# A two-layer streaming encoder in float32: output products of the feed-forward groups issued later, and silu of the gate in one ScalarE instruction

## The chip, the cores and the metric

The kernel runs on one core of one Trainium2 chip. A core has five engines, each with its own queue of instructions that it works through in order: TensorE (PE in the profile; its weight loads are PEld), VectorE (DVE), ScalarE (ACT), GpSimd (POOL) and SyncE (SP), which here only issues DMA transfers. The engines wait for each other by semaphores. The metric is the device time of one execution in microseconds (us), lower is better. The runs of one kernel here lie within 1.1% of each other.

## The reference

All products are in float32 with an accuracy that one pass of the fast format of TensorE does not give, so the kernel makes three products of high and low parts for each. What is computed, for two layers, with x of 512 tokens by 1024:

```
for i in range(DEPTH):                       # 2
    xn = rmsnorm(x, norm1_g[i])
    proj = xn @ w_in[i]                      # 1024 x 6144
    u_pool, q, k, v, g_a, g_b = split(proj)
    o = diff_attention(rotary(rmsnorm(q)), rotary(rmsnorm(k)), v, lam)   # chunk-causal, 4 heads of 2 parts
    attn_out = rmsnorm(o, subln_g[i]) * (1 - lam_init)
    pool_out = pool_mixer(u_pool, pool_w[i], pool_scale[i])              # windowed means, 4 groups
    merged = sigmoid(g_a) * pool_out + sigmoid(g_b) * attn_out
    x = x + merged @ w_out[i]                # 1024 x 1024
    hn = rmsnorm(x, norm2_g[i])
    gate, up = split(hn @ w_ffn_in[i])       # 1024 x 5632
    x = x + (silu(gate) * up) @ w_ffn_out[i] # 2816 x 1024
```

The parts that the change touches are the last three lines, the product with `w_out` ahead of them, and the first lines of the second layer.

## The kernel before

**High and low parts.** Each float32 operand is split into a high part in the fast format and the rest (`split`: ScalarE casts `whi`, VectorE subtracts to `wlo`). A product is three matmuls, high by high, high by low and low by high (`three`, `product`, `in_turn`; L280 to L282 and L299 to L301), each 128 by 128 by 512. Weights come in pieces of 512 KB (`raw`, 7 buffers), and their parts lie in 6 buffers each. With `by_dma`, `parts` makes the low part without VectorE: ScalarE writes minus the high part (L235), and a GpSimd DMA adds the weights to it (L236).

**The residual** `res` lies transposed, 8 rows of tiles by 512 tokens. `add_out` (L685) adds a finished product in PSUM to it.

**Feed-forward.** The 2816 hidden columns are 22 blocks of 128. The last two make the odd group (`odd_group`); the other 20 make five groups of four (`GROUPS`). A group computes its gate and up products by a scheme of seven products instead of eight (`PRODUCTS`, in the order 1, 5, 6, 2, 7, 4, 3), in which sums and differences of weights are made on VectorE (L860 for product 5, L866 and L867 for 6, L880 for 3). Products 1 and 2 add up in the banks named `sc`, 5 and 3 in `tr`, 6 and 7 in `mm`; 4 is in `sc` again. Each product is 24 matmuls.

**Hidden activations.** After products 2, 7, 4 and 3 `Hidden.put` makes h = silu(gate) * up for two tiles of 128 tokens: ScalarE takes tanh of half the normalised gate (`th`, L782), VectorE forms (th + 1) * gate (L783) and multiplies by up and by the factor of the tokens (`h`, L784). Since tokens stand on partitions there and the next product needs hidden columns on partitions, `turned` transposes: VectorE turns blocks of 32 (L314), one DMA writes them to HBM (`away`, L315), four DMAs read them back in place (`near`, L317). `back` splits `near` into `fh` (ScalarE) and `fl` (VectorE). It is emitted by `later`, after a delay in columns of matmuls (`HIDDEN_AWAY`), or at the latest when `need` asks for it. The delays and the order of the code set the order of each queue; the framework's scheduler may move an instruction up where its operands are free.

**Output units.** An output unit is a quarter of the product of a group's hidden activations with `w_ffn_out` (`pair_units`), or a half of the odd group's (`odd_units`): 24 matmuls as well, in two halves whose banks are `oy` and `mm` in turn. Units of a group are issued between the products of the next one, behind products 6, 2, 7 and 4 (`FILLED`); in the last group only two are, and the other two and the last group's four follow at the end. `weight_plan` lists the pieces of weights in the same order, since SyncE loads them in that order.

**Around it.** `last_out` ends the product with `w_out` in four steps, each followed by `Sets.put`, which prepares the input of the feed-forward (`xg`, `xh`, `xl`, and squares `sq`). In the second layer the first attention block needs the root mean square of each token, `token_stats`: VectorE adds the squares, eight tiny matmuls with ones sum them over partitions (L412), and a few small operations follow. It stands behind the first of four products with the weights of q and k.

Of the kernel before, what the change touches and what calls it, by code (L numbers as in the profile page):

```python
# [13 lines left out]
AF = mybir.ActivationFunctionType  # L14
ALU = mybir.AluOpType
# [7 lines left out]
NT = S // P  # L23
# [18 lines left out]
LOADS = {1: ((0, 0),), 5: ((1, 0), (1, 4)), 2: ((0, 4),), 4: ((1, 4),)}  # L42
FILLED = (6, 2, 7, 4)
ODD = 20
# [8 lines left out]
QK_AWAY, SCORE_AWAY, PROB_AWAY, AV_AWAY, MERGE_AWAY = 28000, 26000, 32000, 18000, 24000  # L53
HIDDEN_AWAY = 22000


def weight_plan():
# [22 lines left out]
    for layer in range(L):  # L80
# [24 lines left out]
        for g, f0 in enumerate(GROUPS):  # L105
            for n in PRODUCTS:
                for q in LOADS.get(n, ()):
                    for h in range(2):
                        quarter(f0, *q, h)
                if n in FILLED:  # L110
                    at = FILLED.index(n)
                    if not g:
                        if at < 2:
                            block("w_ffn_out", layer, span((512 * at, 512)), ODD, ODD + 2)
                    elif g < len(GROUPS) - 1 or at < 2:
                        out(GROUPS[g - 1], (at,))
        out(GROUPS[-2], (2, 3))
        out(GROUPS[-1], range(4))
# [4 lines left out]
def trunk_kernel(  # L123
# [278 lines left out]

    def token_stats(full):

# [4 lines left out]
        squares[0] = None  # L409
        ss = mm_ps()[:, :NT]  # L410
        for t in range(NT):
# [60 lines left out]
    for layer in range(L):  # L472
# [14 lines left out]
        def attention(j, before, then):  # L487
# [88 lines left out]
            if not at_start:  # L576
                w = wblock(KD)
            for t in range(NT):
                if at_start:
                    acc = first_acc[t]  # L580
                    first_products(t, steps[2] + steps[3])
                    if not t:
                        token_stats(True)
                else:
                    acc = mm_ps()
                    product(acc, list(zip(x_tok(t), w)))
                    if layer and not t and j == ORDER[0]:
                        token_stats(True)
                qn = sb.tile([P, 4, QK], F32, name="qn", tag="qn", bufs=3)
                ss = small("ss4", 4)  # L590
                for h in range(4):
                    nc.scalar.activation(qn[:, h, :], acc[:, h * QK:(h + 1) * QK], AF.Square, accum_out=ss[:, h:h + 1])
                r = rsqrt_mean(ss, QK, 4, (QK ** -0.5, 1.0), [stats[0][:, i, t:t + 1] for i in (3, 4)])
                for h in range(4):
                    g = qkg[layer][:, h // 2 * QK:(h // 2 + 1) * QK]
                    nc.vector.scalar_tensor_tensor(
                        qn[:, h, :], acc[:, h * QK:(h + 1) * QK], r[:, h:h + 1], g, op0=ALU.mult, op1=ALU.mult)
                rotate(qn, t)
                if not at_start:
                    qn = turned(qn.rearrange("p h c -> p (h c)"), 4, "qn", 3)  # L600
                later(17400 + 5700 * t if at_start else QK_AWAY, lambda t=t, qn=qn: turn(t, qn))
                if not t and then is not None:
                    then()
# [149 lines left out]
        def last_out(x):  # L753
            for i in range(4):
                w = piece(4, True)
                for a in range(2):
                    acc = mm_ps()
                    in_turn(acc, [(cols(w, a)[2 * n + h], (ms[j][0][:, h, :], ms[j][1][:, h, :]))
                                  for n, j in enumerate(ORDER[2:]) for h in range(2)])
                    add_out(i + 4 * a, acc)  # L760
                x.put(i)
# [3 lines left out]
        class Hidden:  # L765
# [9 lines left out]
            def put(self, half, t, gate, up):  # L775

                if half not in self.h:
# [3 lines left out]
                th = sb.tile([P, VD], F32, name="th", tag="mt", bufs=3)  # L781
                nc.scalar.activation(th, gate, AF.Tanh, scale=stats[0][:, 2, n:n + 1])  # L782
                nc.vector.scalar_tensor_tensor(th, th, 1.0, gate, op0=ALU.add, op1=ALU.mult)  # L783
                nc.vector.scalar_tensor_tensor(  # L784
                    h[:, :, t, :], th.rearrange("p (i c) -> p i c", i=2), stats[0][:, 5, n:n + 1],
                    up.rearrange("p (i c) -> p i c", i=2), op0=ALU.mult, op1=ALU.mult)
                if t:
# [9 lines left out]
        def odd_group(x):  # L797
            to = Hidden(ODD, *HIDDEN_AT[ODD])
            w = [piece(2, True) for _ in range(4)]
            accs = [mm_ps(), mm_ps(), tr_ps(), tr_ps()]  # L800
# [40 lines left out]
        def group(g, x):  # L841
# [8 lines left out]
            def prepare(n):  # L850
# [4 lines left out]
                elif n == 5:  # L855
                    raws[21], raws[1] = got
                    sets[5] = []
                    for h in range(2):
                        s1, r21 = raws[1][h][0], raws[21][h][0]
                        nc.vector.tensor_add(s1, r21, s1)  # L860
                        sets[5].append(parts(s1))
# [30 lines left out]
            for n in PRODUCTS:  # L892
# [36 lines left out]
                elif n == 3:  # L929
                    multiply(3, c, False)  # L930
                    for t in range(2):
                        nc.vector.tensor_add(x2[t], c[t], x2[t])
                        to[0].put(1, t, x2[t][:, :VD], x2[t][:, VD:])
                if n in FILLED:
                    at = FILLED.index(n)
                    if not g:
                        if at < 2:
                            odd_units(at)
                    elif g < len(GROUPS) - 1 or at < 2:
                        pair_units(GROUPS[g - 1], at)  # L940

# [31 lines left out]
        for g in range(len(GROUPS)):  # L973
            group(g, sets_of_x)
        for i in (2, 3):
            pair_units(GROUPS[-2], i)
# [59 lines left out]
```

## Time and profile before

| | us |
|---|---|
| median of 3 runs | 1509.73 (1505.37 to 1521.37) |
| the profiled execution | 1509.37 |
| its span, first to last instruction | 1507.6 |
| ScalarE busy / VectorE busy | 700.9 / 1059.6 |
| mean clock granted to TensorE | 0.967 of full speed |

The profiled execution is one run taken by the hardware profiler. A row of a group of instructions gives the line of the code, the engine, the operation with what it writes and reads, how often it ran, and its mean time. A row of a wait gives who waited for whom, the total, how often, and the longest. A row of the timeline gives start, duration and, in brackets, the engine's idle time just before and what ended it. Busy time of TensorE is modelled from the starts of pipelined matmuls; a matmul of 512 columns shows as 0.39 us but the next one starts 0.23 us later.

### The profile page before, as it was taken

The page shows a single profiled execution, that of the slowest core. Times are in us where ns is not written, and L with a number is a line of the kernel's source. Part 1 is how long each engine was busy: PE and PEld are TensorE (multiplying, and loading weights), DVE is VectorE, ACT ScalarE, POOL GpSimd, SP SyncE. Part 2 cuts the span into 40 slices and gives each one's busy share as a digit, 9 for nine tenths or more (in the row PEclk, how much of TensorE's full clock was granted, in tenths as well). Part 3 has the DMA queues.
Part 4 walks back from the last instruction along what each step waited for, and adds up shares of the span by engine and source line. Part 5 has one row for each costly group of instructions (what it writes and reads, how often), then busy time and mean ns, then how long its engine had stood idle before and what let it go on. Part 6 is the DMA issues. An engine that isn't in the chain of part 4 may idle for free.

```text
span 1507.6 us, 18715 instructions
## 1 busy us (share of the span) xinstructions
PE 1414.3 (94%) x6242; PEld 1156.8 (77%) x6242; DVE 1059.6 (70%) x2055; ACT 700.9 (46%) x1310; POOL 129.0 (9%) x151
## 2 busy tenths in 40 slices
PE   9999999997888989898899999999998989898898
PEld 7888888886776867677678888888876767686686
DVE  7778687856756767575667797878576667585763
ACT  6453353455534444454344443535574443553540
POOL 1001000010100000000011101000110000000000
PEclk9999999998989999999999999999999999999999
DMA  8344444465666675757525454445566666757652
GB/s 291 100 141 138 145 138 131 146 155 139 150 171 194 171 205 149 218 158 211 160 65 159 121 178 159 126 133 158 147 154 167 175 187 169 216 149 222 159 162 84
DMA packets 145392, 241.30 MB, mean 160 GB/s; under 512 B 41360, under 2 KB 88976, under 8 KB 145296
## 3 DMA queue, kind: packets, MB, share of 16 engines
q1 hardware_dynamic: 133056, 198.14, 41.1%
q0 software_dynamic: 10944, 39.85, 14.4%
q10 hardware_dynamic: 1296, 2.12, 0.5%
q8 instruction: 49, 0.80, 0.2%
q14 instruction: 47, 0.39, 0.1%
HBM read 210.82 MB, written 29.23 MB: 159 GB/s over the span
## 4 chain that ended last, share of the span: by engine, by line
PE 64%; DMA 15%; DVE 11%; ACT 4%; issue 3%; SPq 2%; POOL 0%; ACTq 0%; DVEq 0%; POOLq 0%
PE mm L299 12%; PE mm L300 12%; PE mm L301 12%; DMA near<-away 8%; DMA away<-near 5%; DMA raw<-in_wts 3%; PE mm L280 3%; PE mm L281 3%; PE mm L282 3%; DVE wlo L211 2%; PE oy L280 2%; PE oy L281 2%; SPq L317 2%; PE oy L282 2%; PE sc L280 2%
## 5 line engine op out<-in xcount | busy, mean ns | idle before, releaser
L210 ACT CAST whi<-raw 128x1024 fp32r<-128x1024 f32 (+1 forms) x229 | 238.1, 1046 | 219.8 <-PE mm L281 87.5
L211 DVE TENSOR_TENSOR wlo<-raw,whi 128x1024 fp32r<-128x1024 f32 (+1 forms) x229 | 275.5, 1210 | 39.0 <-ACT whi L210 38.3
L299 PE MATMUL mm<-whi,xh 128*128 128x512 f32 x480 | 189.9, 396 | 0.0
L301 PE MATMUL mm<-whi,xl 128*128 128x512 f32 x480 | 188.2, 392 | 0.0
L300 PE MATMUL mm<-wlo,xh 128*128 128x512 f32 x480 | 188.1, 392 | 0.0
L280 PE MATMUL oy<-fh,whi 128*128 128x512 f32 (+1 forms) x180 | 80.2, 446 | 65.6 <-ACT fh L210 62.9
L236 POOL DMA_DIRECT2D wlo<-in_wts x76 | 66.6, 876 | 676.8 <-ACT wlo L235 631.4
L301 PEld LDWEIGHTS mm<-whi,xl 128*128 128x128 f32 x480 | 90.7, 189 | 19.4
L300 PEld LDWEIGHTS mm<-wlo,xh 128*128 128x128 f32 x480 | 90.9, 189 | 17.6
L299 PEld LDWEIGHTS mm<-whi,xh 128*128 128x128 f32 x480 | 90.9, 189 | 17.6
L685 DVE TENSOR_TENSOR res<-mm,res 128x512 f32<-128x512 f32 x96 | 65.0, 681 | 53.2 <-PE mm L282 49.0
L333 POOL TENSOR_TENSOR r<-r,mhalf 128x4 f32<-128x4 f32 (+1 forms) x64 | 58.0, 906 | 515.6 <-DVE r L332 442.6
L300 PE MATMUL mm<-xl,whi 128*128 128x512 f32 x256 | 99.8, 390 | 0.0
L299 PE MATMUL mm<-xh,whi 128*128 128x512 f32 x256 | 99.8, 390 | 0.0
L301 PE MATMUL mm<-xh,wlo 128*128 128x512 f32 x256 | 99.6, 389 | 0.0
L280 PEld LDWEIGHTS oy<-fh,whi 128*128 128x128 f32 x180 | 38.6, 215 | 79.4 <-ACT fh L210 68.0
L234 ACT CAST whi<-raw 128x1024 fp32r<-128x1024 f32 x76 | 79.3, 1043 | 37.5 <-PE mm L281 35.4
L280 PE MATMUL sc<-whi,xh 128*128 128x512 f32 x240 | 93.6, 390 | 0.0
L282 PE MATMUL sc<-whi,xl 128*128 128x512 f32 x240 | 93.4, 389 | 0.0
L281 PE MATMUL sc<-wlo,xh 128*128 128x512 f32 x240 | 93.4, 389 | 0.0
L235 ACT ACTIVATE wlo<-raw 128x1024 fp32r<-128x1024 f32 x76 | 80.4, 1057 | 25.1 <-PE sc L281 8.6
L281 PE MATMUL oy<-fl,whi 128*128 128x512 f32 (+1 forms) x180 | 79.4, 441 | 0.2 <-DVE fl L211 0.2
(241 smaller groups left out, 3188.9 us busy)
## 6 DMA issues: line engine op xcount, KB each, us to landing
raw<-in_wts SPq DMA_DIRECT2D x264, 512.0 KB, 4.5
wlo<-in_wts POOLq DMA_DIRECT2D x76, 512.0 KB, 8.1
away<-near SPq DMA_DIRECT2D x72, 256.0 KB, 2.2
near<-away SPq DMA_DIRECT2D x288, 64.0 KB, 2.7
away<-near SPq DMA_DIRECT2D x28, 128.0 KB, 1.7
near<-away SPq DMA_DIRECT2D x112, 32.0 KB, 2.4
res<-in_x_t SPq DMA_DIRECT2D x4, 512.0 KB, 7.0
pwr<-in_pool_w ACTq DMA_DIRECT2D x8, 256.0 KB, 2.7
```

The costliest lines, as they stand in the source:

```text
L210: ins = nc.scalar.copy(hi, src)
L211: nc.vector.tensor_sub(lo, src, hi.bitcast(F32))
L234: nc.scalar.copy(hi, raw)
L235: nc.scalar.activation(lo, raw, AF.Copy, scale=-1.0)
L236: nc.gpsimd.dma_start(lo.rearrange("p a b -> p (a b)"), wts[piece_no], accum_op=ALU.add)
L280: nc.tensor.matmul(acc, lhsT=ah, rhs=bh, start=start, stop=False, **check)
L281: nc.tensor.matmul(acc, lhsT=ah, rhs=bl, start=False, stop=False, **check)
L282: last = nc.tensor.matmul(acc, lhsT=al, rhs=bh, start=False, stop=stop, **check)
L299: nc.tensor.matmul(acc, lhsT=ah, rhs=bh, start=i == 0, stop=False)
L300: nc.tensor.matmul(acc, lhsT=ah, rhs=bl, start=False, stop=False)
L301: last = nc.tensor.matmul(acc, lhsT=al, rhs=bh, start=False, stop=i == n - 1)
L685: return nc.vector.tensor_add(res[d][:, cs], acc, res[d][:, cs])
```

## The change

Six things change.

- Output units are placed by a table, `UNITS`, from the place (group number, product) to the units issued behind it; source -1 is the odd group. Units of group g now begin behind product 4 of group g + 1, and the last two are issued behind products 1 and 5 of group g + 2. The odd group's are behind products 7 and 4 of the first group. At the end all four units of the last but one group and the four of the last stand in a row. `weight_plan` follows.
- `HIDDEN_AWAY` is 42000 columns, not 22000.
- `put` takes silu in one ScalarE instruction, and one VectorE operation multiplies by up and by the factor. ScalarE's table of functions is loaded where silu begins and where exp comes back.
- The pieces of `last_out`, and two of four of the odd group, are split by ScalarE and VectorE, without the GpSimd DMA.
- The first sums of weights in group 0 (L860) are ordered behind the last `add_out` of `last_out`.
- In layer 1 `token_stats` stands behind the second product, in a bank `sc`, and the first tile is evicted after it.

```diff
-FILLED = (6, 2, 7, 4)
+UNITS = {(0, 7): [(-1, 0)], (0, 4): [(-1, 1)], (1, 4): [(0, 0)], (1, 3): [(0, 1)],
+         (2, 1): [(0, 2)], (2, 5): [(0, 3)], (2, 4): [(1, 0)], (2, 3): [(1, 1)],
...
-HIDDEN_AWAY = 22000
+HIDDEN_AWAY = 42000
...
-        out(GROUPS[-2], (2, 3))
+        out(GROUPS[-2], range(4))
...
-    def token_stats(full):
+    def token_stats(full, bank=mm_ps):
...
-        ss = mm_ps()[:, :NT]
+        ss = bank()[:, :NT]
...
-                    if layer and not t and j == ORDER[0]:
-                        token_stats(True)
+                    if layer and j == ORDER[0] and t < 2:
+                        held.append((t, acc))
+                        if not t:
+                            continue
+                        token_stats(True, s_ps)
+                        evicted(*held.pop(0))
+                evicted(t, acc)
...
-                w = piece(4, True)
+                w = piece(4)
...
-                    add_out(i + 4 * a, acc)
+                    x.added = add_out(i + 4 * a, acc)
...
-                nc.scalar.activation(th, gate, AF.Tanh, scale=stats[0][:, 2, n:n + 1])
-                nc.vector.scalar_tensor_tensor(th, th, 1.0, gate, op0=ALU.add, op1=ALU.mult)
+                nc.scalar.activation(th, gate, AF.Silu, scale=stats[0][:, 1, n:n + 1])
                 nc.vector.scalar_tensor_tensor(
-                    h[:, :, t, :], th.rearrange("p (i c) -> p i c", i=2), stats[0][:, 5, n:n + 1],
-                    up.rearrange("p (i c) -> p i c", i=2), op0=ALU.mult, op1=ALU.mult)
+                    h[:, :, t, :], up.rearrange("p (i c) -> p i c", i=2), stats[0][:, 1, n:n + 1],
+                    th.rearrange("p (i c) -> p i c", i=2), op0=ALU.mult, op1=ALU.mult)
...
-            w = [piece(2, True) for _ in range(4)]
+            w = [piece(2, k % 2 > 0) for k in range(4)]
...
-                        nc.vector.tensor_add(s1, r21, s1)
+                        with ExitStack() if g else tc.issue_after(x.added.ins):
+                            nc.vector.tensor_add(s1, r21, s1)
...
-                if n in FILLED:
-                    at = FILLED.index(n)
-                    if not g:
-                        if at < 2:
-                            odd_units(at)
-                    elif g < len(GROUPS) - 1 or at < 2:
-                        pair_units(GROUPS[g - 1], at)
+                for source, i in UNITS.get((g, n), ()):
+                    if source < 0:
+                        odd_units(i)
+                    else:
+                        pair_units(GROUPS[source], i)
```

Where instructions stand in the built programs, at three places. The line numbers of the new kernel are up to ten higher.

TensorE's queue, a middle group of layer 0, around the first output unit on the hidden part that was finished last. Before, behind product 6 (`mm<-...xr`):

```order
L280 MATMUL mm<-whi,xrh 128x512
L281 MATMUL mm<-wlo,xrh 128x512
L282 MATMUL mm<-whi,xrl 128x512
L280 MATMUL oy<-fh,whi 128x512
L281 MATMUL oy<-fl,whi 128x512
L282 MATMUL oy<-fh,wlo 128x512
```

and now, behind product 4 (`sc<-...x`):

```order
L281 MATMUL sc<-whi,xh 128x512
L282 MATMUL sc<-wlo,xh 128x512
L283 MATMUL sc<-whi,xl 128x512
L281 MATMUL oy<-fh,whi 128x512
L282 MATMUL oy<-fl,whi 128x512
L283 MATMUL oy<-fh,wlo 128x512
```

The unit moved down by products 2, 7 and 4 and by two units of the group before.

VectorE's queue, a middle group of layer 0, from the work behind product 3 to the first evictions of units (`res<-oy`, `res<-mm`). Before:

```order
L211 TENSOR_TENSOR fl<-near,fh 128x512
L314 STREAM_TRANSPOSE near<-h 128x4x4x32
L211 TENSOR_TENSOR wlo<-raw,whi 128x1024 x2
L880 TENSOR_TENSOR raw<-raw 128x1024 x2
L211 TENSOR_TENSOR wlo<-raw,whi 128x1024 x2
L211 TENSOR_TENSOR fl<-near,fh 128x512
L906 TENSOR_TENSOR cqn<-mm,cta 128x512 x2
L211 TENSOR_TENSOR wlo<-raw,whi 128x1024
L685 TENSOR_TENSOR res_85<-oy,res_85 128x512
```

and now, from the unit behind product 3 to those behind products 1 and 5:

```order
L695 TENSOR_TENSOR res_86<-mm,res_86 128x512
L876 TENSOR_TENSOR raw<-raw 128x1024
L212 TENSOR_TENSOR wlo<-raw,whi 128x1024
L877 TENSOR_TENSOR raw<-raw 128x1024
L212 TENSOR_TENSOR wlo<-raw,whi 128x1024 x2
L212 TENSOR_TENSOR fl<-near,fh 128x512
L695 TENSOR_TENSOR res_87<-oy,res_87 128x512
L695 TENSOR_TENSOR res_87<-mm,res_87 128x512
L890 TENSOR_TENSOR raw<-raw 128x1024 x2
L212 TENSOR_TENSOR wlo<-raw,whi 128x1024
L695 TENSOR_TENSOR res_88<-oy,res_88 128x512
```

The `fl` of product 3's hidden part stood ahead of the first sums of product 6; now it stands ahead of the eviction of the unit behind product 1.

VectorE's queue in `last_out` of layer 0, from the first eviction on. Before:

```order
L685 TENSOR_TENSOR res_85<-mm,res_85 128x512
L860 TENSOR_TENSOR raw<-raw 128x1024
L211 TENSOR_TENSOR xl<-xg,xh 128x512
L685 TENSOR_TENSOR res_87<-mm,res_87 128x512
L717 TENSOR_TENSOR xg<-xg 128x256
```

and now:

```order
L695 TENSOR_TENSOR res_85<-mm,res_85 128x512
L212 TENSOR_TENSOR xl<-xg,xh 128x512
L695 TENSOR_TENSOR res_87<-mm,res_87 128x512
L212 TENSOR_TENSOR wlo<-raw,whi 128x1024
L727 TENSOR_TENSOR xg<-xg 128x256
```

L860 (now L870) left the place behind the first eviction; it follows the last one of `last_out`, and a split of a piece of the odd group's weights stands among the evictions.

More of the change, by code (lines that the diff above doesn't have):

```diff
@@ L109, in weight_plan @@
                         quarter(f0, *q, h)
-                if n in FILLED:
-                    at = FILLED.index(n)
-                    if not g:
-                        if at < 2:
-                            block("w_ffn_out", layer, span((512 * at, 512)), ODD, ODD + 2)
-                    elif g < len(GROUPS) - 1 or at < 2:
-                        out(GROUPS[g - 1], (at,))
-        out(GROUPS[-2], (2, 3))
+                for source, i in UNITS.get((g, n), ()):
+                    if source < 0:
+                        block("w_ffn_out", layer, span((512 * i, 512)), ODD, ODD + 2)
+                    else:
+                        out(GROUPS[source], (i,))
+        out(GROUPS[-2], range(4))
         out(GROUPS[-1], range(4))
@@ L577, in attention, with evicted @@
                 w = wblock(KD)
[L578 to L582, printed above, removed]
-                        token_stats(True)
-                else:
-                    acc = mm_ps()
-                    product(acc, list(zip(x_tok(t), w)))
-                    if layer and not t and j == ORDER[0]:
-                        token_stats(True)
+            held = []
+            def evicted(t, acc):
                 qn = sb.tile([P, 4, QK], F32, name="qn", tag="qn", bufs=3)
@@ L601, in attention @@
                 later(17400 + 5700 * t if at_start else QK_AWAY, lambda t=t, qn=qn: turn(t, qn))
+            for t in range(NT):
+                if at_start:
+                    acc = first_acc[t]
+                    first_products(t, steps[2] + steps[3])
+                    if not t:
+                        token_stats(True)
+                else:
+                    acc = mm_ps()
+                    product(acc, list(zip(x_tok(t), w)))
+                    if layer and j == ORDER[0] and t < 2:
+                        held.append((t, acc))
+                        if not t:
+                            continue
+                        token_stats(True, s_ps)
+                        evicted(*held.pop(0))
+                evicted(t, acc)
                 if not t and then is not None:
@@ L933, in group @@
                         to[0].put(1, t, x2[t][:, :VD], x2[t][:, VD:])
[L934 to L937, printed above, removed]
-                            odd_units(at)
-                    elif g < len(GROUPS) - 1 or at < 2:
-                        pair_units(GROUPS[g - 1], at)
+                for source, i in UNITS.get((g, n), ()):
+                    if source < 0:
+                        odd_units(i)
+                    else:
+                        pair_units(GROUPS[source], i)
         def next_x(i):
@@ L974, in trunk_kernel @@
             group(g, sets_of_x)
-        for i in (2, 3):
+        for i in range(4):
             pair_units(GROUPS[-2], i)
```

2 rows, old and new, of the table UNITS are left out of this document.

## The prediction

> **What bounds the kernel now.** I read the page first, then TensorE's own waits, then the clock just behind each of them, then the chain of waits at two places.
>
> ```profile
> span 1507.6 us, 18715 instructions
> ...
> PE 1414.3 (94%) x6242; PEld 1156.8 (77%) x6242; DVE 1059.6 (70%) x2055; ACT 700.9 (46%) x1310; POOL 129.0 (9%) x151
> ```
>
> TensorE is busy 94% of the span, so 1507.6 - 1414.3 = 93 us of idle time is one thing to win. The other hides inside "busy": after a wait the granted clock falls, and the matmuls behind it take longer. The waits of TensorE alone (total, how often, longest; the smaller ones left out add to 6.4 us):
>
> ```profile
> PE oy L280 <- ACT fh L210: 62.9, 12, 7.6
> PE mm L280 <- DVE res L685: 12.1, 4, 8.5
> PE mm L412 <- DVE sq L408: 2.9, 1, 2.9
> PE oy L280 <- DVE res L685: 2.7, 2, 1.7
> PE tr L280 <- DVE cqn L932: 2.5, 5, 0.8
> ```
>
> So one kind of wait, an output unit waiting for the hidden activations `fh`, makes two thirds of the idle time. What the clock adds I read from stretches of 7 us that start where TensorE resumes (columns: stretch, busy time and count by engine, then the granted clock, DMA share, GB/s):
>
> ```profile
> core 0: us, PE busy (x) PEld busy (x) DVE busy (x) ACT busy (x) POOL busy (x), PEclk, DMA share, GB/s
> 357.90:364.90 7.00, 7.00 (x23) 5.65 (x24) 6.97 (x12) 6.65 (x11) 0.53 (x1) 0.72 0.00 0
> 418.46:425.46 7.00, 7.00 (x20) 5.31 (x21) 2.27 (x4) 0.00 (x0) 0.00 (x0) 0.66 0.18 75
> ...
> 767.75:774.75 7.00, 7.00 (x21) 5.84 (x22) 3.12 (x15) 0.00 (x0) 2.05 (x2) 0.51 0.00 0
> 1109.67:1116.67 7.00, 7.00 (x25) 5.68 (x26) 6.97 (x12) 6.65 (x11) 0.55 (x1) 0.78 0.27 60
> ...
> 1431.99:1438.99 7.00, 7.00 (x20) 5.32 (x21) 3.70 (x5) 0.90 (x1) 0.00 (x0) 0.64 1.01 347
> 1481.60:1488.60 7.00, 6.78 (x28) 5.36 (x29) 2.05 (x3) 0.00 (x0) 0.00 (x0) 1.00 0.10 37
> ```
>
> TensorE is "busy" for all 7 us, yet at clock 0.64 it issues 20 matmuls. A stretch at clock c loses (1 - c) x 7 us. Eleven stretches follow long waits for `fh` (first 418.46, last 1431.99) and lose 25.8 us together, 2.35 each; the twelfth wait, 2.0 us before 1481.60, left the clock at 1.00. The two behind `res` (357.90, 1109.67) lose 3.5 us, the one behind `sq` (767.75) 3.4 us.
>
> **Why the units wait.** The pace: product 6 of a group has eight triples, from the first row here to one pitch behind the second, 5.44 us for 24 matmuls. An output unit has 24 as well.
>
> ```profile
> 405.27 0.39 PE L280 MATMUL mm<-whi,xrh 128*128 128x512 f32 x1
> ...
> 410.03 0.39 PE L280 MATMUL mm<-whi,xrh 128*128 128x512 f32 x1
> ```
>
> The chain of one group (rows of TensorE, SyncE and VectorE, and the chain of waits between them):
>
> ```profile
> 597.17 0.47 PE L280 MATMUL tr<-whi,xth 128*128 128x512 f32 x1 [0.66 <-DVE cqn L932]
> 601.99 0.70 DVE L314 STREAM_TRANSPOSE near<-h 128x512 f32<-128x512 f32 x1
> 602.72 0.34 SPq L315 DMA_DIRECT2D away<-near  x1
> 606.77 6.29 DMA near<-away
> 613.16 0.63 ACT fh L210
> 613.81 0.69 DVE L211 TENSOR_TENSOR fl<-near,fh 128x512 fp32r<-128x512 f32 x1 [1.50 <-ACT fh L210]
> 613.83 0.79 PE L280 MATMUL oy<-fh,whi 128*128 128x512 f32 x1 [4.87 <-ACT fh L210]
> ```
>
> Product 5 could start at 597.17 - 0.66 = 596.51, so product 1 began, and product 3 of the group before ended, at 591.07. Its hidden part is ready at 613.79, 22.7 us later: 11.6 us in VectorE's queue, 10.4 us in two DMA passes, the rest on ScalarE. Between product 3 and the unit lie products 1, 5 and 6, 16.3 us. Where product 5 does not wait (first row below) the same sum gives 16.3 + 5.2 = 21.5 us. The other two rows are waits at the end of layer 0 and of the kernel:
>
> ```profile
> 545.00 0.80 PE L280 MATMUL oy<-fh,whi 128*128 128x512 f32 x1 [5.22 <-ACT fh L210]
> 734.13 0.80 PE L280 MATMUL oy<-fh,whi 128*128 128x512 f32 x1 [4.00 <-ACT fh L210]
> 1481.60 0.50 PE L280 MATMUL oy<-fh,whi 128*128 128x512 f32 x1 [2.02 <-ACT fh L210]
> ```
>
> **The change, part by part.**
>
> Units later. In the groups with all four units the first unit on a group's hidden part moves from behind product 6 (16.3 us after product 3) to behind product 4; between lie units, too: 1, unit, 5, unit, 6, 2, 7, 4, so 8 x 5.44 = 43.5 us against a need of 21.5 to 22.7. The odd group's units move behind products 7 and 4: five products, 27.2 us; the longest wait, 7.6 us past 16.3, means a need of 23.9. At the end four units instead of two cover the last group: 21.8 us against 4.0 us beyond two units and a 1.7 us wait in layer 0, 16.6. All twelve waits go: -62.9, and with them -25.8 of clock. The waits for `cqn` (-2.5) and for `res` at the last units (-2.7) go as well: a unit now lies between product 3 and the next group's product 1, and between 1 and 5.
>
> What is late next: VectorE. Its order puts `fl` of product 3 ahead of the eviction of the unit behind product 1, whose bank `oy` the unit behind product 5 writes. That unit starts 21.8 us after product 3 (unit, 1, unit, 5); before it must lie `fl` 0.69 and the eviction, about 0.7, so `fh` must end by 20.4. It took 21.5 to 22.7: a wait of 1.1 to 2.3, if nothing of the chain gets shorter, in three groups of each layer. Ends: 0 (the loads by accumulation of product 2 are now issued behind `fh`, no longer beside its DMA) to 6.6 each, if `away` takes 5.1 more, as the slow one here against the median:
>
> ```profile
> 402.96 7.30 DMA away<-near
> ...
> away<-near SPq DMA_DIRECT2D x72, 256.0 KB, 2.2
> ```
>
> I take 1.5 x 6 = +9.0, nearest to the measured chain, with no clock price, since 2.0 us had none.
>
> Last output products before the feed-forward. The wait of 8.46 us is no shortage of weights:
>
> ```profile
> 339.28 16.02 DMA raw<-in_wts
> ...
> 355.42 1.23 DVE L860 TENSOR_TENSOR raw<-raw 128x1024 f32<-128x1024 f32 x1 [13.41 <-DMA raw<-in_wts]
> ...
> 357.90 0.79 PE L280 MATMUL mm<-mh,whi 128*128 128x512 f32 x1 [8.46 <-DVE res L685]
> ```
>
> VectorE stands at L860 for a load that landed at 355.3, with the evictions behind it; the new order puts L860 behind the last eviction. Gone: all four waits of this kind, -12.1, and -3.5 of clock. Twelve pieces of weights are split by VectorE, not by a second ScalarE pass and an accumulating DMA:
>
> ```profile
> L211 DVE TENSOR_TENSOR wlo<-raw,whi 128x1024 fp32r<-128x1024 f32 (+1 forms) x229 | 275.5, 1210 | 39.0 <-ACT whi L210 38.3
> L235 ACT ACTIVATE wlo<-raw 128x1024 fp32r<-128x1024 f32 x76 | 80.4, 1057 | 25.1 <-PE sc L281 8.6 <-ACT wlo L235 7.4 <-PE sc L282 2.0
> wlo<-in_wts POOLq DMA_DIRECT2D x76, 512.0 KB, 8.1
> ```
>
> VectorE +12 x 1.21 = 14.5 us, ScalarE -12.7, and 12 DMAs of 512 KB less. Six fall in each layer, 7.3 us, under the 13.4 us for which VectorE stood at L860 in layer 0; cost 0, at most 14.5 if that cover is gone.
>
> Silu. Each layer has 11 hidden pairs with four `put`s each, so 88 of L783 go; ScalarE's instruction keeps its form, and three table loads come (silu, exp, silu):
>
> ```profile
> L782 ACT ACTIVATE th<-cta,stats x20: 508/510/512, 452.5 to 1465.2; 128x256 f32<-128x256 f32 x20
> L783 DVE SCALAR_TENSOR_TENSOR th<-th,cta x20: 378/416/422, 454.0 to 1466.6; 128x256 f32<-128x256 f32 x20
> L375 ACT ACT_TABLE_LOAD  x1: 1283/1283/1283, 1.2 to 1.2; - x1
> 545.00:613.80 68.80, 62.95 (x264) 50.70 (x264) 45.70 (x62) 30.92 (x39) 5.20 (x6) 0.95 0.67 183
> ```
>
> 88 x 0.416 = 36.6 us off VectorE, which is busy 45.7 of 68.8 us in a group: off the path, gain 0, at best 0.8 us per chain (two in a row) where the chain still binds. The loads: 0 to 3 x 1.28 = 3.8; ScalarE is busy 30.9 of 68.8 us, so 0. The Trainium skill, page "ScalarE: Activation LUTs", section "What ACT_TABLE_LOAD costs", speaks against the change here: a switch of set costs the load and a drain, 2.66 us together; our row agrees on the 1283 ns of the load and shows no drain. By that page the three would be up to 8.0 us, and the sum 1411 instead of 1403.
>
> Start of layer 1. The sums of squares are ready 2.92 us after the first product; now a second product (5.44 us) runs first: -2.9 and -3.4 of clock. The price is bank pressure: the first product's bank must be free before the fourth starts, one product after the statistics. Its last reader ends at 773.5 in this row, 5.8 us after they started at 767.75; one product and the statistics themselves (1.5 us) take 6.9: cost 0, at most 2.
>
> ```profile
> 767.75 1.45 PE L412 MATMUL mm<-ones,sq 128*128 128x1 f32 x7 [2.92 <-DVE sq L408]
> 772.40 1.13 DVE L596 SCALAR_TENSOR_TENSOR qn<-mm,r,hg 128x128 f32<-128x128 f32 x4 [1.19 <-POOL r L333]
> ```
>
> The longer delay (42000 for 22000 columns, 18.6 for 9.7 us at 5.44 per 12288) sends the splits to ScalarE later, where it stood long for `near` already; nothing on TensorE asks for them sooner than above: 0.
>
> **The sum.** 62.9 + 25.8 + 2.5 + 2.7 + 12.1 + 3.5 + 2.9 + 3.4 = 115.8. Span 1507.6 - 115.8 + 9.0 = 1400.8; the profiled execution took 1509.37, 1.8 more than its span, so 1402.6, say 1403. The median of the three runs, 1509.73, is the same within 0.4.
>
> **Rivals.**
> - The wait moves to VectorE's queue in full: `fh` ends 5.1 us later than before, six waits of 6.6 with 2.35 of clock, 53.7 instead of 9.0: 1447. For it: a group at full pace takes 11 x 5.44 = 59.8 us for the DMA work of 68.8 (0.67 x 68.8 = 46.1, a share of 0.77). Against: part of that traffic now comes later.
> - The move does nothing for the units: each `fh` is emitted later and stands in ScalarE's queue until its new unit waits as long. Then only 12.1 + 3.5 + 2.9 + 3.4 = 21.9 goes: 1487. Against: 43.5 us of work for a chain of 22.7.
> - The other side, slower: DMA becomes the bound in the groups. Behind the waits the engines run at share 1.01 and 347 GB/s, so they can be filled. The ten groups would then last as long as their DMA work; since 21.9 us are won elsewhere, it decides at 68.8 + 2.2 = 71.0 us a group, 54% more than the 46.1 us of now. At 72 us the time is 1509 + 32 - 22 = 1519. No row here shows packets that much slower.
>
> **How the numbers follow.** Forecast (below 1420) 0.74, the VectorE rival (1420 to 1460) 0.17, units unmoved 0.04, DMA bound 0.02, several of these that cancel to within 1% 0.03. The range goes from 1389 (no residual wait, 1391.8 + 1.8, and most of the 6.4 us of small waits gone) to 1440, into the first rival. A measurement of this kernel tells some 1% from no change; faster by more 0.95, within 0.03, slower 0.02.
>
> **What would show it.** Right: no TensorE wait for `fh` above 2 us; mean clock above 0.985 for 0.967; the wait of `mm` for `res` gone; groups of about 60 us; no wait for `sq`. The residual shows as `oy` waiting for `res`, three times a layer. Wrong: waits for `fh` or `res` of over 4 us with clock 0.64 behind them, a DMA share near 1 through whole groups, or TensorE waiting for `wlo`, `th` or `h`.

## The result, and the profile after

| | before | after |
|---|---|---|
| median, us | 1512.1 (4 runs, 1505.4 to 1521.4) | 1404.1 (4 runs, 1400.3 to 1410.5) |
| profiled execution, us | 1509.4 | 1400.3 |
| its span, us | 1507.6 | 1398.5 |

The ratio is 0.929, with a 95% interval from 0.922 to 0.935: the changed kernel is faster by 108 us. Forecast were 1403 us for the profiled execution, 1389 to 1440. The profiled execution of the changed kernel is the fastest of its four.

The head of the page of the changed kernel (span, busy time of each engine, granted clock in 40 slices):

```profile
span 1398.5 us, 18612 instructions
...
PE 1375.9 (98%) x6242; PEld 1137.6 (81%) x6242; DVE 1045.0 (75%) x1979; ACT 693.4 (50%) x1301; POOL 117.7 (8%) x139
...
PEclk9999999999999999999999999999999999999999
```

Two sums explain the gain. TensorE's idle time fell from 93.3 to 1398.5 - 1375.9 = 22.6 us, 70.7 less. Its busy time, with the same 6242 matmuls, fell by 38.4 us: the matmuls that ran at a low clock behind the waits are at full clock now. The forecast had 74.1 less for the waits (83.1 less the 9.0 that it expected to remain) and 32.7 for the clock.

TensorE's two largest waits in the changed kernel (total us, how often, longest; no other kind adds up to more than 1.7 us):

```profile
PE oy L281 <- DVE res L695: 9.6, 6, 2.5
PE mm L300 <- DVE qn L589: 3.5, 2, 2.4
```

No wait for `fh` is left, none for `sq`, and none of `mm` for `res`. The two rows are what stands in their place. The columns of the next view are those of the prediction's stretches; it has one middle group of layer 0 and the same of layer 1:

```profile
547.03:606.87 59.84, 59.84 (x265) 49.57 (x264) 43.45 (x56) 31.39 (x38) 5.24 (x6) 1.00 0.78 215
...
1247.00:1307.00 60.00, 60.00 (x266) 49.70 (x265) 44.95 (x58) 31.75 (x40) 5.21 (x6) 1.00 0.78 215
```

A group lasts 59.84 us, which is eleven blocks of 24 matmuls at 5.44 us; TensorE is busy for all of it at full clock. The DMA share rose from 0.67 to 0.78, where the first rival had worked out 0.77, and the passes of the chain hardly felt it: the medians from issue to landing are 2.4 us for an `away` DMA (2.2 before) and 2.1 us for a `near` one (2.7 before).

```profile
away<-near SPq DMA_DIRECT2D x72, 256.0 KB, 2.4
near<-away SPq DMA_DIRECT2D x288, 64.0 KB, 2.1
```

The engines beside TensorE still wait for the hidden parts, only nobody waits for them: ScalarE stands 83.2 us for `near`, VectorE 46.9 us at `fl`.

```profile
ACT fh L211: 83.2, 25
DVE fl L212: 46.9, 20
```

### The profile page after: what moved, and what is told of

Its sections match the earlier page's. It is cut to its first block, busy times and chain, and to the rows that moved or that the text cites. A ratio compares the mean times of both kernels' runs of the same rounds, so it can differ in the third digit from the quotient of the medians.

```text
span 1398.5 us, 18612 instructions
## 1 busy us (share of the span) xinstructions
PE 1375.9 (98%) x6242; PEld 1137.6 (81%) x6242; DVE 1045.0 (75%) x1979; ACT 693.4 (50%) x1301; POOL 117.7 (8%) x139
## 4 chain that ended last, share of the span: by engine, by line
PE 81%; DMA 7%; DVE 6%; ACT 2%; issue 1%; SPq 1%; POOL 1%; ACTq 0%; DVEq 0%; POOLq 0%
PE mm L300 13%; PE mm L302 12%; PE mm L301 12%; PE mm L282 6%; PE mm L283 5%; PE mm L281 5%; DMA away<-near 4%; PE oy L281 2%; PE oy L282 2%; PE oy L283 2%; PE sc L281 2%; PE sc L282 2%; PE tr L282 2%; PE tr L283 2%; PE tr L281 2%; PE sc L283 2%
## 5 line engine op out<-in xcount | busy, mean ns | idle before, releaser
L211 ACT CAST whi<-raw 128x1024 fp32r<-128x1024 f32 (+1 forms) x241 | 250.9, 1048 | 197.9 <-PE mm L282 56.8
L212 DVE TENSOR_TENSOR wlo<-raw,whi 128x1024 fp32r<-128x1024 f32 (+1 forms) x241 | 291.3, 1212 | 57.1 <-ACT whi L211 55.8
L237 POOL DMA_DIRECT2D wlo<-in_wts x64 | 56.1, 876 | 561.5 <-ACT wlo L236 336.6
L334 POOL TENSOR_TENSOR r<-r,mhalf 128x1 f32<-128x1 f32 (+1 forms) x64 | 56.7, 887 | 523.4 <-DVE r L333 420.3
L281 PE MATMUL oy<-fh,whi 128*128 128x512 f32 (+1 forms) x180 | 70.3, 391 | 9.7 <-DVE res L695 9.6
L236 ACT ACTIVATE wlo<-raw 128x1024 fp32r<-128x1024 f32 x64 | 67.0, 1056 | 16.3 <-PE mm L282 14.0
L235 ACT CAST whi<-raw 128x1024 fp32r<-128x1024 f32 x64 | 66.6, 1040 | 11.4 <-PE mm L282 7.2
L283 PE MATMUL oy<-fh,wlo 128*128 128x512 f32 (+1 forms) x180 | 69.7, 387 | 0.0
L282 PE MATMUL oy<-fl,whi 128*128 128x512 f32 (+1 forms) x180 | 69.6, 387 | 0.0
```

The source lines that it names most:

```text
L211: ins = nc.scalar.copy(hi, src)
L212: nc.vector.tensor_sub(lo, src, hi.bitcast(F32))
L235: nc.scalar.copy(hi, raw)
L236: nc.scalar.activation(lo, raw, AF.Copy, scale=-1.0)
L281: nc.tensor.matmul(acc, lhsT=ah, rhs=bh, start=start, stop=False, **check)
L282: nc.tensor.matmul(acc, lhsT=ah, rhs=bl, start=False, stop=False, **check)
```

## The experiments

Ratios are against runs of the kernel before on the same chip, with their 95% intervals. The changed kernel itself is at 0.929 (0.922 to 0.935). Where one step is given in us, it is a ratio times the median of before in the same job, 1513 to 1514 us.

### The units alone

The kernel before with the table `UNITS`, its plan of weights and the end loop over four units; nothing else.

```diff
-FILLED = (6, 2, 7, 4)
+UNITS = {(0, 7): [(-1, 0)], (0, 4): [(-1, 1)], (1, 4): [(0, 0)], (1, 3): [(0, 1)],
...
-        for i in (2, 3):
+        for i in range(4):
             pair_units(GROUPS[-2], i)
```

> The kernel before, with nothing changed but the places of the output units (and the order of the weights that belongs to it): tanh, the delay of 22000, the loads by accumulation and the place of the statistics stay as they were. Theory: the units alone carry the terms 62.9 + 25.8 + 2.5 + 2.7 less a residue of about 9, so 1512 - 85 = 1427 us, no wait of TensorE for fh above 2 us, the 8.5 us wait behind res still there. Rival 1: the units gain only together with the longer delay, because with 22000 VectorE stands at fl with the evictions of the units behind it; then 1450 us or more and waits of oy for res in the groups. Rival 2: the move alone does nothing, about 1510 us.

Measured: 1423.9 us, ratio 0.941 (0.938 to 0.944). That is 89.3 us (84.5 to 94.3) for a sum of terms of 84.9. Its waits:

```profile
PE mm L281 <- DVE res L686: 12.5, 3, 8.6
PE oy L281 <- DVE res L686: 7.6, 5, 3.5
PE mm L413 <- DVE sq L409: 2.9, 1, 2.9
```

All waits for `fh` are gone with this edit alone, and the waits that belong to the other edits stand as before. The units are 89 of the 108 us of the change.

### Everything but the units, with both delays

The changed kernel with the old places of the units; first with the delay of 42000 as changed, then with 22000.

```diff
-UNITS = {(0, 7): [(-1, 0)], (0, 4): [(-1, 1)], (1, 4): [(0, 0)], (1, 3): [(0, 1)],
+UNITS = {(0, 6): [(-1, 0)], (0, 2): [(-1, 1)], (1, 6): [(0, 0)], (1, 2): [(0, 1)], (1, 7): [(0, 2)], (1, 4): [(0, 3)],
...
-HIDDEN_AWAY = 42000
+HIDDEN_AWAY = 22000
```

> The changed kernel with the units back in their old places, all else as changed (silu, delay 42000, splits on VectorE, statistics one product later). Theory: the twelve waits for fh and the clock behind them return, less what a shorter chain saves (0.8 us each at most): 1404 + 94 - 10 - 9 to 1404 + 94, so 1479 to 1498 us, with about 63 us of TensorE waiting for fh and a granted clock near 0.65 behind each. Rival: silu and the freed VectorE shortened the chain so much that the old places do nearly as well: below 1440 us.

> The changed kernel with the units in their old places and the delay back at 22000. With the delay of 42000 the same kernel took 1503 us and its waits for fh were 72.5 us, up to 10.6 in the first group, against 62.9 before. Theory: it was the long delay, which leaves several parts of the hidden activations to be made at once when an early unit asks for them; with 22000 the waits fall to 52 to 63 us and the time to 1480 to 1493 us. Rival: the delay has no part in it, 1498 us or more, and what the last output products won is lost again by an earlier start against the same loads.

Measured: 1503.3 us with 42000, ratio 0.992 (0.989 to 0.995), above the range expected; 1493.7 with 22000, ratio 0.988 (0.985 to 0.991), 0.7 us above its range. Waits for `fh`, first with 42000, then with 22000:

```profile
PE oy L281 <- ACT fh L211: 72.5, 12, 10.6
```

```profile
PE oy L281 <- ACT fh L211: 63.8, 12, 8.6
```

With 22000 the waits are those of the kernel before (62.9), so silu and the freed VectorE did not shorten what TensorE waits for. With 42000 the profile has 8.7 us more of them; the times point the same way, but the two intervals overlap, so the long delay as their cause is likely and not proved. The units alone and the kernel without units and longer delay multiply to 0.941 x 0.988 = 0.930. The kernel that holds both of these parts is the changed kernel with a delay of 22000, at 0.934 (0.931 to 0.936, next section); so far as the intervals tell, the two parts do not depend on each other.

### The delay, with the new units

The changed kernel with 22000, and with 56000 columns.

```diff
-HIDDEN_AWAY = 42000
+HIDDEN_AWAY = 22000
```

> The changed kernel with the old delay of 22000 columns for the split of the hidden part. Theory of the prediction: the longer delay is worth nothing on TensorE, 1400 to 1410 us. Rival: with the short delay fl stands in VectorE's queue about 9 us earlier, up to 13 us ahead of the landing of near, and the evictions of the units wait behind it, so that TensorE waits for res several times a group at 2 to 6 us each with a lower clock behind: 1425 us or more, and VectorE's idle time at fl rises from 47 us to over 100.

> The changed kernel with a delay of 56000 columns. Theory: what is left of waits of oy for res comes from fl standing at the head of VectorE's queue until its transfer lands; at 22000 these waits were 20.9 us, at 42000 9.6 us, so at 56000 they fall to 4 to 9 us, fl waits less than 47 us, and the time is 1395 to 1404 us. Rival: the rest is the bank oy asked for again 2.7 us after its unit while VectorE has the sums and splits of the next product ahead, which no delay changes: 1401 to 1407 us with waits of about 9.6 us in the same places.

Measured: 1413.9 us with 22000, ratio 0.934 (0.931 to 0.936); 1404.5 with 56000, ratio 0.928 (0.925 to 0.930). The short delay is slower than the longest one by more than both intervals, some 9 us. Against the changed kernel with its 42000 it is some 7 us, which by itself is not clear of the intervals (0.931 to 0.936 and 0.922 to 0.935). Between 42000 and 56000 the times show no difference. Neither expectation for 22000 was met in full: the waits of `oy` for `res` are of the rival's kind, 20.9 us in seven waits, but they fall in the first three groups of a layer, not in all, and VectorE's idle time at `fl` is 59 us, not over 100. The timeline of VectorE with 22000, where the longest lies, behind product 4 of the first group in layer 1 (start, duration; in brackets the idle time before, and what ended it):

```profile
1127.49 0.48 DVE L793 SCALAR_TENSOR_TENSOR h<-cta,stats,th 128x256 f32<-128x256 f32 x1
1133.46 0.69 DVE L212 TENSOR_TENSOR fl<-near,fh 128x512 fp32r<-128x512 f32 x1 [5.49 <-ACT fh L211]
1134.07 0.48 DVE L793 SCALAR_TENSOR_TENSOR h<-cta,stats,th 128x256 f32<-128x256 f32 x1
1134.46 0.68 DVE L695 TENSOR_TENSOR res<-oy,res 128x512 f32<-128x512 f32 x1
```

```profile
1135.20 0.80 PE L281 MATMUL oy<-fh,whi 128*128 128x512 f32 x1 [9.27 <-DVE res L695]
```

and of the changed kernel at the same place:

```profile
1121.19 0.88 DVE L793 SCALAR_TENSOR_TENSOR h<-cta,stats,th 128x256 f32<-128x256 f32 x2
1121.98 0.68 DVE L695 TENSOR_TENSOR res<-oy,res 128x512 f32<-128x512 f32 x1
...
1123.98 0.69 DVE L212 TENSOR_TENSOR fl<-near,fh 128x512 fp32r<-128x512 f32 x1
```

With the short delay `fl` stands between the two `h` and holds the eviction of `oy` for 5.49 us; TensorE waited 9.27 us for that bank. With 42000 this `fl` comes behind the eviction, and TensorE waits 2.17 us.

The longest delay did not shorten these waits, though its theory had 4 to 9 us. There are six, in the six places where the changed kernel has them, as the rival said, but of 13.0 us for its 9.6:

```profile
PE oy L281 <- DVE res L695: 13.0, 6, 4.9
```

The longest stands at the same place again. Another `fl`, between the sums L870 of the next group, is ahead of this eviction in the queue (VectorE, then TensorE, with 56000):

```profile
1120.35 0.69 DVE L212 TENSOR_TENSOR fl<-near,fh 128x512 fp32r<-128x512 f32 x1 [3.22 <-ACT fh L211]
```

```profile
1127.09 0.80 PE L281 MATMUL oy<-fh,whi 128*128 128x512 f32 x1 [4.88 <-DVE res L695]
```

From there to the eviction VectorE works without a pause. This `fl` starts 1.02 us after the unit (1119.33), and in the changed kernel 1.69 us ahead of it (1115.98 and 1117.67): 2.71 us later, by which the wait is longer, 4.88 for 2.17. So the delay decides about one `fl` at this place and leaves the other as it is.

### Silu

Tanh and two VectorE operations in the changed kernel; and, the other way round, silu alone in the kernel before.

```diff
-                nc.scalar.activation(th, gate, AF.Silu, scale=stats[0][:, 1, n:n + 1])
+                nc.scalar.activation(th, gate, AF.Tanh, scale=stats[0][:, 2, n:n + 1])
+                nc.vector.scalar_tensor_tensor(th, th, 1.0, gate, op0=ALU.add, op1=ALU.mult)
...
```

> The changed kernel with tanh on ScalarE and two operations on VectorE again. Theory: VectorE's 36.6 us were off the path, so 1402 to 1408 us; the six waits of oy for res, 9.6 us in all, grow by the 0.4 to 0.8 us that stand ahead of the late evictions, at most 5 us together. Rival: VectorE is so close to the bound now that the groups run at 98% that the 36.6 us show in full or in half: 1420 us or more, with oy waiting for res in every group.

> The kernel before with silu alone: one instruction on ScalarE, one on VectorE, nothing else changed. Theory: VectorE is off the path, but the chain that TensorE waits for there holds two of the removed operations, so each of the twelve waits for fh gets up to 0.8 us shorter: 1502 to 1513 us. Rival 1: 36.6 us off VectorE show in full, 1480 us or less. Rival 2: three more table loads stand in that chain, 1513 to 1520 us.

Measured: 1408.6 us with tanh back, ratio 0.931 (0.928 to 0.933), 0.6 us above the range of its theory, far from the rival's 1420, and not to be told from the changed kernel. Silu alone: 1512.4 us, ratio 0.999 (0.9976 to 1.0005), inside the range of its theory. Some 30 us less of VectorE's busy time (1059.6 to 1029.6 us in the profile of silu alone) are worth between -1 and 4 us. Its waits for `fh`:

```profile
PE oy L280 <- ACT fh L210: 64.1, 12, 9.3
```

64.1 us against 62.9: the 0.8 us per wait that the chain could have won do not show.

### The last output products: the hold and the pieces

First without the hold on the sum for product 5, then with the twelve pieces by accumulating DMA again, then both.

```diff
-                        with ExitStack() if g else tc.issue_after(x.added.ins):
-                            nc.vector.tensor_add(s1, r21, s1)
+                        nc.vector.tensor_add(s1, r21, s1)
```

```diff
-                w = piece(4)
+                w = piece(4, True)
...
-            w = [piece(2, k % 2 > 0) for k in range(4)]
+            w = [piece(2, True) for k in range(4)]
```

> The changed kernel without the one hold that keeps the sum for product 5 of group 0 behind the last eviction of the output products. Theory: VectorE stands again at that sum, for a load, with the evictions behind it; the term 12.1 + 3.5 comes back in full or in good part, 1412 to 1420 us, and TensorE waits for res at the last output products, 6 us or more in layer 0. Rival: the wait of before came from the pieces of weights split with an accumulating DMA, which are on VectorE now; then at most 1407 us and no such wait.

> The changed kernel with the twelve weight pieces of the last output products and of the odd group made by ScalarE and an accumulating DMA again. Theory: the 14.5 us on VectorE lie under time in which it stands, so the edit is worth 0, 1400 to 1408 us. Rival 1: the edit was what removed the wait for res there, so 1412 us or more and that wait is back. Rival 2: the 14.5 us cost something now, so the kernel gets faster by 3 us or more, 1393 to 1400 us, through shorter waits of oy for res in group 0, which follows.

> The changed kernel without the hold and with the twelve pieces by accumulating DMA again, the two edits that each alone could be undone at no cost. Theory formed on those runs: either of them is enough to keep the evictions of the last output products from standing behind a sum that waits for its load; with both undone VectorE stands some 13 us at that sum again, TensorE waits about 8 us for res near the end of the first attention stage, and the term of 12.1 + 3.5 comes back, less what pieces off VectorE give: 1410 to 1420 us. Rival: something else of the change (silu, the delay, the units) moved the loads, then still no such wait and 1400 to 1406 us.

Measured: without the hold 1405.9 us, ratio 0.929 (0.926 to 0.932); with the pieces back 1402.1 us, ratio 0.927 (0.923 to 0.930); with both 1424.2 us, ratio 0.940 (0.937 to 0.942). The first expectation missed, and the rival's time and waits came: the hold can go at no cost. The second held, also at no cost. Only both together bring the term back: 0.9396 - 0.9291 = 0.0105 or 15.9 us against the first, 0.0128 or 19.4 us against the second, with some 7 us of uncertainty each (half widths of the two intervals added in squares); 15.6 were forecast. The time with both is 4 us above the range expected, the wait of about 8 us is as expected, and the waits of `mm` for `res` are 12.0 us, for 12.1 before. The profile with both is of its fastest execution, 1413.8 us, 10 us under the median, so it does not show all that the other executions lost.

VectorE at the sum (L869 in these two), without the hold:

```profile
343.80 1.23 DVE L869 TENSOR_TENSOR raw<-raw 128x1024 f32<-128x1024 f32 x1 [1.22 <-DMA raw<-in_wts]
344.95 0.68 DVE L695 TENSOR_TENSOR res<-mm,res 128x512 f32<-128x512 f32 x1
```

and with both undone, with TensorE's wait behind it:

```profile
356.87 1.23 DVE L869 TENSOR_TENSOR raw<-raw 128x1024 f32<-128x1024 f32 x1 [13.82 <-DMA raw<-in_wts]
358.61 0.69 DVE L695 TENSOR_TENSOR res<-mm,res 128x512 f32<-128x512 f32 x1
```

```profile
359.35 0.79 PE L281 MATMUL mm<-mh,whi 128*128 128x512 f32 x1 [8.85 <-DVE res L695]
```

The sum stands ahead of the evictions in both (with both undone, of all but the first). With the pieces on VectorE its load has landed 13 us earlier, so the place in the queue does no harm. Most of these 13 us are in the transfer: the load is issued at 338.12 and takes 5.6 us without the hold, and is issued at 340.32 and takes 16.4 us with both undone. In this stretch, 315 to 362 us, the accumulating DMAs (`wlo<-in_wts`) are two and five, and the last column, the median from issue to landing, rises for the loads (first without the hold, then with both undone):

```profile
raw<-in_wts SPq DMA_DIRECT2D x9, 512.0 KB, 4.5
wlo<-in_wts POOLq DMA_DIRECT2D x2, 512.0 KB, 7.6
```

```profile
raw<-in_wts SPq DMA_DIRECT2D x7, 512.0 KB, 10.4
wlo<-in_wts POOLq DMA_DIRECT2D x5, 512.0 KB, 9.1
```

So there are two cures for one wait: take the sum out of the way, or have its load early by leaving out the accumulating DMAs beside it.

### The statistics of the second layer

```diff
-                    if layer and j == ORDER[0] and t < 2:
-                        held.append((t, acc))
...
-                        token_stats(True, s_ps)
...
+                    if layer and not t and j == ORDER[0]:
+                        token_stats(True)
```

> The changed kernel with the token statistics of layer 1 behind the first product again, in the bank they had. Theory: the wait for sq of 2.9 us and 3.4 us of lower clock return, and what the change pays there (two waits for qn, 3.5 us in all) goes: 1404 + 6.3 - 3.5 to 1404 + 6.3, so 1406 to 1411 us. Rival: the move gains nothing or loses, since the bank pressure takes back what the wait gave: 1400 to 1405 us.

Measured: 1404.8 us, ratio 0.928 (0.925 to 0.931), in the rival's range. No difference shows, but the two intervals leave some 10 us open, so the times alone would not exclude the 6.3 us that were forecast. The waits say more. With the old place:

```profile
PE mm L413 <- DVE sq L409: 2.9, 1, 2.9
...
PE mm L300 <- DVE qn L597: 0.6, 1, 0.6
```

and the two of the changed kernel that are not there (or shorter):

```profile
734.14 0.47 PE L300 MATMUL mm<-whi,xh 128*128 128x512 f32 x1 [1.03 <-DVE qn L589]
```

```profile
842.78 0.47 PE L300 MATMUL mm<-mh,whi 128*128 128x512 f32 x1 [2.43 <-DVE qn L589]
```

2.9 us of one wait were traded for 1.03 + 2.43 - 0.61 = 2.85 us of two others. The first is the bank pressure that the prediction bounded at 2. The second lies 109 us later, at the first of the products with `w_out` that stand inside attention; all ten profiles with the new place have it, and the four with the old place do not. Since the statistics no longer take a bank of the `mm` rotation, every later product there has its neighbour's bank; that this is the way from cause to effect was not tried by itself.

### A version meant to be faster

The units are written ahead of the operations that take up the product they stand behind, so that their evictions come earlier in VectorE's queue.

```diff
+            def out_units(n):
+                for source, i in UNITS.get((g, n), ()):
...
                     multiply(4, a)
+                    out_units(4)
...
                     multiply(3, c, False)
+                    out_units(3)
...
```

> The changed kernel with the output units written ahead of the operations that take up the product they stand behind, so that on VectorE the eviction of a unit stands ahead of more of the hidden part's work. Theory: the six waits of oy for res, 9.6 us, are a matter of VectorE's order alone and go in good part: 1394 to 1400 us. Rival: the hidden parts come later by up to 5.4 us and new waits for fh or for tr take the place: 1404 us or more.

Measured: 1406.7 us, ratio 0.930 (0.927 to 0.933). The waits moved rather than went: one of 6.9 us for `res`, and new ones for weights. The one of 6.9 us is behind product 4 of the first group of layer 1 once more; VectorE stands 6.53 us at the `fl` between the sums L870, ahead of that eviction.

```profile
PE oy L281 <- DVE res L695: 10.0, 5, 6.9
...
PE sc L282 <- DMA wlo<-in_wts: 2.6, 2, 1.3
PE oy L281 <- ACT whi L211: 1.6, 1, 1.6
```

The theory missed. The rival's time came, but not the waits for `fh` or `tr` that it named. None of the versions tried is faster than the changed kernel by more than the measurement tells.

## Why the prediction was right, and where it was not

**The units: right.** 84.9 us forecast for the terms 62.9 + 25.8 + 2.5 + 2.7 less 9.0, 89.3 (84.5 to 94.3) measured alone. The second rival (units unmoved in effect, 1487) is excluded by the same run; the other parts without units and delay took about its time, 1493.7. The first rival's wait of 6.6 us in VectorE's queue did not come.

**What remained: the size right, the place wrong.** The sum had six waits of 1.5 us where the unit behind product 5 asks for `oy`, on the chain "if nothing of the chain gets shorter". It got shorter. In the changed kernel product 3 of a middle group ends at 601.43 us, where the unit behind it starts (TensorE, VectorE, SyncE and ScalarE in order of time):

```profile
601.43 0.39 PE L281 MATMUL oy<-fh,whi 128*128 128x512 f32 x1
...
609.37 0.70 DVE L315 STREAM_TRANSPOSE near<-h 128x512 f32<-128x512 f32 x1
610.10 0.33 SPq L316 DMA_DIRECT2D away<-near  x1
...
616.69 0.62 ACT L211 CAST fh<-near 128x512 fp32r<-128x512 f32 x1 [0.95 <-DMA near<-away]
617.34 0.69 DVE L212 TENSOR_TENSOR fl<-near,fh 128x512 fp32r<-128x512 f32 x1 [0.34 <-ACT fh L211]
617.95 0.68 DVE L695 TENSOR_TENSOR res<-oy,res 128x512 f32<-128x512 f32 x1
...
623.19 0.39 PE L281 MATMUL oy<-fh,whi 128*128 128x512 f32 x1
```

`fh` is done at 617.31, 15.9 us after product 3, not 21.5 to 22.7, and `fl` at 618.03; the passes from `away` to `fh` take 6.6 us instead of 10.4. The order is the forecast one, `fl` just ahead of the eviction, but the bank is free at 618.63 and asked for at 623.19. No wait stands at any of the six places, so they came out at the lower end that the prediction had named, 0. The 9.6 us that are there come from the same kind of queue at places the sum did not look at: behind products 7 and 4 of the first group, where the odd group's units use `oy` every 2.7 us, and behind product 1 of the third group (layer 0; the same three places wait 0.94, 2.17 and 2.53 us in layer 1):

```profile
413.70 0.50 PE L281 MATMUL oy<-fh,whi 128*128 128x512 f32 x1 [0.43 <-DVE res L695]
...
426.88 0.50 PE L281 MATMUL oy<-fh,whi 128*128 128x512 f32 x1 [2.00 <-DVE res L695]
...
492.51 0.47 PE L281 MATMUL oy<-fh,whi 128*128 128x512 f32 x1 [1.51 <-DVE res L695]
```

That the total is near 9.0, in three waits a layer as forecast, is chance.

**The last output products: the size right, one cause of two.** "VectorE stands at L860 for a load, with the evictions behind it" is what the runs show, at 15.9 to 19.4 us for a forecast of 15.6. But the prediction credited the new order alone and put the pieces at a cost of 0 with no gain, though the slow load of its own row, 16.02 us, is one that they cure. Either edit is enough; each is worth 0 only as long as the other is there.

**The start of layer 1: wrong.** The terms -2.9 and -3.4 do not show in the time, and the waits show why: 2.9 us were won and 2.85 paid. The step that failed is "cost 0, at most 2": the second wait for `qn`, 2.43 us, was outside the stretch that the prediction looked at. The lower clock of 3.4 us was 1.7 in the run with the old place (0.76 over the 7 us behind `sq`, for 0.51 in the kernel before).

```profile
706.12:713.12 7.00, 7.00 (x28) 5.76 (x29) 3.56 (x15) 0.00 (x0) 2.04 (x2) 0.76 0.00 0
```

**The longer delay: wrong.** "Nothing on TensorE asks for them sooner: 0" looked at who needs `fh`, not at who stands behind `fl` in VectorE's queue. With the new units a delay of 22000 costs some 9 us against 56000 (against 42000 some 7, not clear of the intervals), and with it one `fl` holds an eviction for 5.49 us.

**Silu: right at 0**, between -1 and 4 us in the kernel before. The cost of the pieces shows as 0 too, within some 11 us. The bound of 0.8 us per chain was not even reached in the kernel where the chain does bind. The switch to silu in the changed kernel, on ScalarE:

```profile
382.44 1.05 ACT L211 CAST whi<-raw 128x1024 fp32r<-128x1024 f32 x1 [0.50 <-PE tr L283]
383.50 1.28 ACT L792 ACT_TABLE_LOAD   x1
384.80 0.84 ACT L792 ACTIVATE th<-mm,stats 128x256 f32<-128x256 f32 x2
```

The load starts where the cast ends, and the first silu 1.30 us later. The other two switches of the kernel look the same, with less than 0.02 us of idle time on either side of the load. The Trainium skill, page "ScalarE: Activation LUTs", section "What ACT_TABLE_LOAD costs", has a drain besides the load at every switch; three switches would be up to 8.0 us by an estimate from its figures. The trace agrees on the load and shows no drain. The time, 1.6 us below before with silu alone, shows no such cost either, but ScalarE is busy for 47% of that run, so it could be hidden.

**The total: right by parts that cancel.** The forecast had 6.3 us too much for layer 1; the units gave 4.4 us more than their terms and the last output products 0.3 to 3.8. Each of these, and the share of the delay, is within the uncertainty of the times. That the total came within 3 us of the forecast is in part luck.

## What to carry to other kernels

When an engine at 94% waits in a regular pattern, add up the lead that the program gives to each product and compare it with the chain behind the wait, measured step by step; more lead was worth 89 us here, and taking two operations out of the chain nothing. Then look at every queue in which the moved work now stands: what waits there for a transfer, and which eviction is behind it. A wait with two cures shows nothing when either is undone alone, so undo them together before crediting one.

## What the runs showed of the hardware that was not expected

The length of a wait does not by itself tell what clock follows. The same wait of 2.42 to 2.43 us for `qn` at the same matmul stands in ten of the profiles. In five the next 7 us are at full clock, in five at 0.76, which is 1.7 us lost. First the changed kernel, then the one with a delay of 56000:

```profile
842.78:849.78 7.00, 7.00 (x31) 5.79 (x32) 6.18 (x12) 1.36 (x2) 0.00 (x0) 1.00 0.49 154
```

```profile
842.38:849.38 7.00, 7.00 (x24) 5.62 (x25) 5.25 (x11) 1.36 (x2) 0.00 (x0) 0.76 0.39 112
```

Over all fourteen profiles, TensorE waits of 1.3 to 1.82 us were never followed by a lower clock (19 of them), waits from 1.83 to 2.8 us sometimes were, and all of 2.9 us or more were, to 0.51 to 0.80 over the next 7 us, with no order by their length. The prediction's "no clock price, since 2.0 us had none" held in the profiled execution, and is no rule. This goes with the times of the changed kernel: its four executions have granted clocks of 1.0, 0.998, 0.996 and 0.995 for 1400, 1403, 1405 and 1411 us. The Trainium skill, page "TensorE: Matmul & The Clock Gate", section "HAM oscillation — how this bites in real kernels", asks only for gaps above some 3.4 us to be avoided. These runs disagree, since a lower clock followed gaps of 1.83 to 2.8 us in a part of the cases and every gap from 2.9 us on.

A load of weights beside accumulating DMAs was slow: the same 512 KB landed 16.4 us after issue in the run whose stretch held five of them, and 5.6 us in the run with two.
